# Recurrence keys turned in 32x32 blocks on VectorE and put in place through DRAM, instead of turned on TensorE

## The chip, the cores and the metric

The kernel runs on one core of a Trainium2 chip. Its time is the device time of one execution in microseconds (us). The time of the kernel before is the median of three runs. The trace and the page of the profile come from one execution of their own, which was timed too.

## The reference, cut to what matters

One encoder block over 1024 tokens of width 1024, all in float32. After a layer norm, one wide projection gives the inputs of a dilated attention and of a gated linear recurrence (HGRN2) with eight heads that runs over the tokens forwards and backwards. Both results are merged and projected, and a gated feed-forward layer follows. The change lies in the recurrence. Of it, this part needs the keys with tokens along the contraction:

```python
cum = jnp.cumsum(logf.reshape(b, h, n, c, kd), axis=3)
q_dec = q * jnp.exp(cum)
k_inv = k * jnp.exp(-cum)
a = jnp.einsum('bhnik,bhnjk->bhnij', q_dec, k_inv)
...
u = jnp.einsum('bhnck,bhncv->bhnkv', k * jnp.exp(cum_last - cum), v)
...
_, s_start = lax.scan(step, init, (jnp.moveaxis(decay, 2, 0), jnp.moveaxis(u, 2, 0)))
```

`u` is summed over the tokens `c` of a chunk. It is what the states are made of.

## The kernel before

**Stages.** The first stage computes the projection (11776 columns) and, beside it, attention and recurrence; later stages compute the merge, the output projection and the feed-forward layer. The first stage lasts from the start to about 1190 us; the recurrence's heads lie between 110 and 930 us of it.

**The stream of products.** `stream` yields 322 products. One product is twelve matmuls of 128x128 by 128x512 (four blocks of the contraction, three parts of a split float32 product: lines 277, 278, 279, called by `mm3`). Each yield of `stream` is one *slot*; slots and products are counted alike here, from 0. After certain products a result leaves PSUM (`leave`, at once by priority) through VectorE or ScalarE into a tile `evh`, and SyncE stores that tile to DRAM (lines 578, 598, 609, 628).

**The side work.** In `phase1` the loop over `stream` moves a second generator, one unit at a time: `hgrn_side` for each of eight heads, and attention. A number that `hgrn_side` yields is the number of slots until it is taken up again. A unit starts when its inputs have been produced. Slots give a priority; the scheduler of the framework then sets a fixed order of instructions for each engine. At run time each engine works through its order and waits where an input isn't there.

**One head.** `hgrn_dir` (two directions, `d` 0 and 1) makes the decayed queries `qd` and keys `ki` in place in tile `t` with ScalarE, VectorE (scans, line 1189; reciprocals, line 1207) and GpSimd (line 1197, and line 1210, which finishes the keys). A tile `t` holds eight chunks of 128 tokens as keys x tokens. `hgrn_keys` turns each half of four chunks with four TensorE transposes (line 1224, moving operand the identity in `tabs_sb`) into one PSUM tile `sd`, and ScalarE copies it to `hkT` (line 1225). `hgrn_states` multiplies the turned keys with the values `hv` (line 1240, four and three chunks a direction; the trace has two records for each of these matmuls), scales them on ScalarE (line 1242) and chains them on VectorE and ScalarE (lines 1248, 1251). `hgrn_scores` and `hgrn_out` follow. In slots from the head's start: the keys of direction 0 are turned in slot 4, its states and the turning of direction 1 stand in slot 7, the states of direction 1 in slot 10, the scores in 13, the outputs in 16.

**Queues.** Nearly all DMAs are issued by SyncE (SP) in order: the weight blocks `wa` (line 256), the stores of `evh`, the read-backs of what was stored. A DMA that waits for its input holds up all that stand behind it in SP's order. The instructions of `hgrn_side` that issue DMAs are the fetch of `hv` at its start and of `hg` (line 816) in slot 9.

Of the kernel before, what the change touches and what calls it, by code (L numbers as in the profile page):

```python
# [10 lines left out]
F32 = mybir.dt.float32  # L11
# [11 lines left out]
HALF = 512  # L23
# [56 lines left out]
class Block:  # L80
    evac_ahead = 1000

    def __init__(self, ctx, tc, x, ln_in_g, ln_in_b, w_in, hgrn_lb, hgrn_norm_g, w_att_up, w_hgrn_up,
                 w_o, ln1_g, ln1_b, w_ffn_in, w_ffn_out, ln2_g, ln2_b, tabs, out, dbg=None):
        self.tc, self.nc, self.ctx = tc, tc.nc, ctx
        self.x = x[0]
        self.ln = {"in": (ln_in_g, ln_in_b), "1": (ln1_g[0], ln1_b[0]), "2": (ln2_g[0], ln2_b[0])}
        self.w_in, self.lbw, self.ng = w_in[0], hgrn_lb, hgrn_norm_g[0]
        self.wa, self.wr, self.wo = w_att_up[0], w_hgrn_up[0], w_o[0]
        self.wfi, self.wfo, self.tabs, self.out = w_ffn_in[0], w_ffn_out[0], tabs, out[0]  # L90
        self.dbg = dbg or {}
        nc = self.nc

        self.npj = 0
        self.issued = {}
        self.psum = ctx.enter_context(tc.tile_pool(name="psum", bufs=1, space=PSUM))
        self.cst = ctx.enter_context(tc.tile_pool(name="cst", bufs=1))
        self.tiny = ctx.enter_context(tc.tile_pool(name="tiny", bufs=1))
        self.spare = self.pad(self.cst, CST_PAD)
        self.wpool = self.pool("wp", "right")  # L100
        self.wp = self.wpool.__enter__()
        dram = ctx.enter_context(tc.tile_pool(name="dram", bufs=1, space=DRAM))

        def scratch(name, n):
            if name in self.dbg:
                return [self.dbg[name][i] for i in range(n)]
            return [dram.tile([128, 1024], F32, name=f"{name}{i}") for i in range(n)]

        self.att_d = scratch("att", 4)
        self.rec_d = scratch("rec", 8)  # L110
        self.tg_d = scratch("tg", 16)
        self.n1_d = scratch("n1", 8)
        self.ahs_d = scratch("ahs", 8)
        self.hg_d = [{n: dram.tile([128, T], F32, name=f"hg{h}{n}") for n in ("t0", "t1", "q")}
                     for h in range(8)]
        self.at_d = [{(k, g): dram.tile([128, T], F32, name=f"at{j}{k}{g}") for k in "qk" for g in range(3)}
                     for j in range(4)]
        for h in range(8):
            self.hg_d[h].update({n: dram.tile([T, 128], F32, name=f"hg{h}{n}") for n in "vg"})
        for j in range(4):  # L120
            self.at_d[j].update({("v", g): dram.tile([T, 128], F32, name=f"at{j}v{g}") for g in range(3)})
        self.w_d = [dram.tile([32, 128], F32, name=f"wd{j}") for j in range(4)]
        self.td = [dram.tile([128, 4, HALF], F32, name=f"td{i}") for i in range(3)]
        self.gd = {p: dram.tile([128, NF // 2, HALF], F32, name=f"gd{p}") for p in range(1, 8)}
        self.consts()
# [686 lines left out]
    def fetch_rows(self, n, name, src, g=0):  # L812
# [14 lines left out]
                        self.nc.sync.dma_start(t.rearrange("p (r e) d -> p r e d", e=2)[p:p + 32, :, e], z[i, h, e])  # L827
        return t

    def att_small(self, n, w=8):  # L830
        return self.smt.tile([128, 2, w], F32, name=n, tag=n, bufs=1)

# [382 lines left out]
        nc.vector.scalar_tensor_tensor(qd[:, :, near], q3[:, :, near], CQ, qd[:, :, near], op0=OP.mult, op1=OP.mult)  # L1215
        yield

    def hgrn_keys(self, st, d):

        nc, out = self.nc, []  # L1220
        for b in (0, 1) if d == 0 else (1, 0):
            pt, kT = self.ps_sd(), self.half3("hkT")
            for k in range(4):
                nc.tensor.transpose(pt[:, 128 * k:128 * (k + 1)], st["ki", d][:, 4 * b + k, :], self.ident)
            nc.scalar.copy(kT, pt.rearrange("p (k c) -> p k c", k=4))
            out.append(kT)
        return out

    def hgrn_states(self, st, d, kT, vT):


        nc, dec = self.nc, st["dec", d]
        S = self.slot(6 + d, "hS", (8, 128))
        cs = list(range(8)) if d == 0 else list(range(7, -1, -1))
        E = None
        for b in range(2):
# [4 lines left out]
            for jj, c, after in part:  # L1241
                nc.scalar.activation(S[:, after, :], ps[:, jj, :], AF.Copy, scale=dec[:, 0, c:c + 1])
            for jj, c, after in part:
                if E is None:
                    E = S[:, after, :]
                else:
                    En = self.sm.tile([128, 128], F32, name="hR", tag="hR", bufs=3)
                    nc.vector.scalar_tensor_tensor(En, E, dec[:, 2, c:c + 1], S[:, after, :], op0=OP.mult, op1=OP.add)
                    E = En
                if after != cs[1]:  # L1250
                    nc.scalar.activation(S[:, after, :], E, AF.Copy, scale=dec[:, 1, after:after + 1])
                    if after == cs[2]:
                        nc.scalar.activation(S[:, cs[1], :], S[:, cs[1], :], AF.Copy, scale=dec[:, 1, cs[1]:cs[1] + 1])
        return S
# [55 lines left out]
    def hgrn_side(self, h, st):  # L1310
        nc = self.nc
        vT = self.fetch_rows(5, "hv", self.hg_d[h]["v"])
        st["fa"] = self.slot(6, "fa")
        steps = [self.hgrn_dir(h, d, st) for d in range(2)]
        for _ in range(2):
            for z in steps:
                next(z)
                yield 1
        k0 = self.hgrn_keys(st, 0)
        for z in steps:  # L1320
            next(z)
        yield 2
        next(steps[0])
        yield 1
        S = {0: self.hgrn_states(st, 0, k0, vT)}
        k1 = self.hgrn_keys(st, 1)
        yield 2
        next(steps[1])
        sg = self.fetch_rows(8, "hg", self.hg_d[h]["g"])
        yield 1  # L1330
        S[1] = self.hgrn_states(st, 1, k1, vT)
        yield 3
        am = [self.hgrn_scores(st, b) for b in range(2)]
        yield -3
        for b in range(2):
            self.hgrn_out(h, st, b, am[b], vT, S, sg)
# [743 lines left out]
```

## Time and profile before

| | |
|---|---|
| median of 3 runs | 2018.45 us (2018.29 to 2022.23) |
| the profiled execution | 2016.14 us |
| its span, first to last instruction | 2014.3 us |
| ScalarE busy | 932.8 us (46%) |
| GpSimd busy | 990.4 us (49%) |
| DMA packets | 416125, 301.17 MB, of them under 512 B 133153 |

How to read the rows of the profile shown below. PE is TensorE (PEld its weight loads, which overlap it), DVE is VectorE, ACT is ScalarE, POOL is GpSimd, SP is SyncE, and a `q` behind an engine's name means its sequencer, as where it issues a DMA. A row of the timeline gives start and duration in us, engine, source line, operation, output and inputs, and how many like it were merged. Matmuls overlap, so their durations add to more than the time from one start to the next. A row of waits gives who waited for whom, us in total, how often, and the longest. A row of groups gives busy us and mean ns of one, then the idle time of the engine before them. A row of DMA issues gives count, KB each and the median us from issue to landing. A row of windows gives the stretch, then busy us (and instructions) of PE, PEld, DVE, ACT and POOL, the clock granted to TensorE (1.00 is full speed), the busy share of the 16 DMA engines and GB/s.

### The profile page before, as it was taken

How to read it: one execution, taken by the hardware profiler on the slowest of the kernel's cores; microseconds unless marked ns; L12 is line 12 of the kernel's file. 1: busy time of each engine (PE TensorE's matmuls, PEld its weight loads, DVE VectorE, ACT ScalarE, POOL GpSimd, SP SyncE). 2: the span in 40 equal slices, each digit the busy share in tenths (PEclk: the TensorE clock that was granted, in tenths of full speed). 3: DMA queues.
4: the chain of work that ended last, by engine and by line, in shares of the span. 5: the costliest groups of instructions: out<-in, count | busy, mean ns of one | idle time of the engine just before them, and what ended most of it. 6: DMA issues, size and time to landing. Idle time of an engine off the chain costs nothing. (4 is left out here: it accounts for less than half of the span.)

```text
span 2014.3 us, 30896 instructions
## 1 busy us (share of the span) xinstructions
PE 1976.9 (98%) x10718; PEld 1637.0 (81%) x10718; DVE 1360.7 (68%) x2225; ACT 932.8 (46%) x1926; POOL 990.4 (49%) x866
## 2 busy tenths in 40 slices
PE   7999999999999999999999999999999999999998
PEld 5688788888888888888888878887788888888886
DVE  7877646895478855786443256558777776767788
ACT  6654455553645546455554333345333333344541
POOL 6566643665456654566546422244666665620000
PEclk9999999999999999999999999999999999999999
DMA  5545555456455454555546377534434443447533
GB/s 162 141 126 141 155 131 147 134 126 174 114 153 138 133 155 118 151 156 152 141 121 196 117 256 233 158 119 141 142 125 136 147 136 126 146 163 277 167 103 122
DMA packets 416125, 301.17 MB, mean 150 GB/s; under 512 B 133153, under 2 KB 359394, under 8 KB 415970
## 3 DMA queue, kind: packets, MB, share of 16 engines
q1 hardware_dynamic: 410624, 282.14, 47.9%
q10 hardware_dynamic: 5346, 17.08, 2.3%
q8 instruction: 84, 1.38, 0.3%
q14 instruction: 71, 0.58, 0.1%
HBM read 204.96 MB, written 94.18 MB: 149 GB/s over the span
## 5 line engine op out<-in xcount | busy, mean ns | idle before, releaser
L229 POOL TENSOR_TENSOR w_lo<-wa,w_hi 128x512 fp32r<-128x512 f32 x272 | 366.0, 1355 | 247.3 <-ACT w_hi L219 231.2
L219 ACT CAST w_hi<-wa 128x512 fp32r<-128x512 f32 x272 | 168.2, 620 | 232.4 <-PE pj L278 150.5
L229 POOL TENSOR_TENSOR w_lo<-wsum,w_hi 128x512 fp32r<-128x512 f32 x88 | 127.6, 1460 | 111.2 <-PE sd L279 60.7
L229 POOL TENSOR_TENSOR w_lo<-f_raw,w_hi 128x512 fp32r<-128x512 f32 x66 | 101.1, 1540 | 51.8 <-ACT w_hi L219 50.7
L215 POOL TENSOR_TENSOR mv<-mv,mhalf 128x1 f32<-128x1 f32 x16 | 12.6, 790 | 221.7 <-DVE mv L214 218.7
L219 ACT CAST w_hi<-wsum 128x512 fp32r<-128x512 f32 x88 | 54.5, 621 | 116.5 <-PE sd L278 106.7
L219 ACT CAST gwsum<-a_raw 128x512 fp32r<-128x512 f32 (+1 forms) x78 | 48.2, 618 | 112.2 <-PE pj L278 55.5
L277 PE MATMUL pj<-xt1hi,w_hi 128*128 128x512 f32 x252 | 99.3, 394 | 0.7 <-DVE evh L589 0.7
L607 DVE TENSOR_TENSOR evh<-wkeep,pj 128x512 f32<-128x512 f32 x45 | 30.9, 686 | 99.9 <-PE pj L279 60.1
L278 PE MATMUL pj<-xt1lo,w_hi 128*128 128x512 f32 x252 | 98.3, 390 | 0.0
L279 PE MATMUL pj<-xt1hi,w_lo 128*128 128x512 f32 x252 | 98.1, 390 | 0.0
L727 POOL TENSOR_TENSOR wa<-wa,wa 128x512 f32<-128x512 f32 x46 | 66.8, 1452 | 58.5 <-DVE wa L726 55.2
L229 POOL TENSOR_TENSOR w_lo<-ws,w_hi 128x512 fp32r<-128x512 f32 x46 | 62.1, 1352 | 61.7 <-ACT w_hi L219 57.8
L755 ACT COPY wkeep<-pj 128x512 f32<-128x512 f32 x136 | 79.4, 584 | 0.1
L229 DVE TENSOR_TENSOR gwkeep<-a_raw,gwsum 128x512 fp32r<-128x512 f32 (+1 forms) x78 | 53.0, 680 | 36.5 <-ACT gwsum L219 33.6
L279 PE MATMUL pj<-xt2hi,w_lo 128*128 128x512 f32 x192 | 75.3, 392 | 1.7 <-POOL w_lo L229 1.7
L277 PE MATMUL pj<-xt2hi,w_hi 128*128 128x512 f32 x192 | 75.9, 396 | 0.8 <-ACT w_hi L219 0.8
L278 PE MATMUL pj<-xt2lo,w_hi 128*128 128x512 f32 x192 | 75.5, 393 | 1.2 <-DVE xt2lo L409 1.0
L229 POOL TENSOR_TENSOR w_lo<-w_raw,w_hi 128x512 fp32r<-128x512 f32 x24 | 33.5, 1398 | 87.8 <-ACT w_hi L219 87.8
L277 PE MATMUL pj<-xt4hi,w_hi 128*128 128x512 f32 x192 | 75.9, 395 | 0.0
L278 PE MATMUL pj<-xt4lo,w_hi 128*128 128x512 f32 x192 | 75.3, 392 | 0.0
L278 PE MATMUL pj<-xb11lo,w_hi 128*128 128x512 f32 x192 | 75.3, 393 | 0.0
(440 smaller groups left out, 6536.2 us busy)
## 6 DMA issues: line engine op xcount, KB each, us to landing
wa<-in_w_in_dram SPq DMA_DIRECT2D x184, 256.0 KB, 3.4
f_raw<-in_w_ffn_in_dram SPq DMA_DIRECT2D x44, 512.0 KB, 4.3
a_raw<-gd SPq DMA_DIRECT2D x30, 512.0 KB, 3.9
gd<-fc SPq DMA_DIRECT2D x44, 256.0 KB, 2.0
gd<-fs SPq DMA_DIRECT2D x33, 256.0 KB, 2.2
tg<-evh SPq DMA_DIRECT2D x32, 256.0 KB, 3.4
tg<-tg SPq DMA_DIRECT2D x16, 512.0 KB, 4.8
y<-ahs SPq DMA_DIRECT2D x16, 512.0 KB, 7.5
```

Source lines behind the costliest of these rows:

```text
L215: nc.gpsimd.tensor_tensor(mv[:, 2:3], mv[:, 2:3], self.mhalf[:, 0:1], OP.pow)
L219: ins = nc.scalar.copy(hi, src) if eng_hi == "act" else nc.vector.tensor_copy(hi, src)
L229: ins = e.tensor_sub(lo, src, hi.bitcast(F32))
L277: nc.tensor.matmul(ps, whi, xhi, start=first, stop=False, **kw)
L278: nc.tensor.matmul(ps, whi, xlo, start=False, stop=False, **kw)
L279: self.product = nc.tensor.matmul(ps, wlo, xhi, start=False, stop=last, **kw).ins.name
L607: self.left(nc.vector.tensor_add(t, add, ps))
L727: nc.gpsimd.tensor_sub(a["a21"], a["a22"], a["a11"])
L755: nc.scalar.copy(t, ps)
```

## The change

`hgrn_keys` no longer uses TensorE, PSUM and ScalarE. VectorE turns each half of `t` in 32x32 blocks (`flipped`, one instruction of 128x512), which turns every block but leaves the blocks where they were. The tile is stored to a DRAM scratch `kd` as it is (`stored`, 256 KB) and read back into itself by four DMAs (`back`, 64 KB each), one for each band of 32 partitions, in runs of 32 numbers (128 B), so that the blocks come to their places. For the 16 directions these are 32 such turns, 32 stores and 128 read-backs.

The slots of a head change with it. The keys are turned in slot 3 (direction 0) and 4 (direction 1), stored in slots 4 and 5, read back in 6 and 7; the states stand in slots 10 and 12, the scores in 15, the outputs in 18.

```diff
+        self.kd = [[dram.tile([128, HALF], F32, name=f"kd{h}{n}") for n in range(4)] for h in range(8)]
...
+    def flipped(self, t, scr, src=None):
+
+        self.nc.vector.transpose(t, t if src is None else src)
+        return t, scr
+
+    def stored(self, flips):
+        for t, scr in flips:
+            self.nc.sync.dma_start(scr, t)
+
+    def back(self, flips):
+        for t, scr in flips:
+            z = scr.rearrange("(a i) (k b j) -> b i k a j", a=4, b=4, j=32)
+            for b in range(4):
+                self.nc.sync.dma_start(t[32 * b:32 * b + 32, :].rearrange("i (k a j) -> i k a j", a=4, j=32), z[b])
...
-    def hgrn_keys(self, st, d):
-
-        nc, out = self.nc, []
-        for b in (0, 1) if d == 0 else (1, 0):
-            pt, kT = self.ps_sd(), self.half3("hkT")
-            for k in range(4):
-                nc.tensor.transpose(pt[:, 128 * k:128 * (k + 1)], st["ki", d][:, 4 * b + k, :], self.ident)
-            nc.scalar.copy(kT, pt.rearrange("p (k c) -> p k c", k=4))
-            out.append(kT)
-        return out
+    def hgrn_keys(self, h, st, d):
+        return [self.flipped(self.half("hkT"), self.kd[h][2 * d + b],
+                             st["ki", d][:, 4 * b:4 * b + 4, :].rearrange("p k c -> p (k c)"))
+                for b in ((0, 1) if d == 0 else (1, 0))]
...
-        for _ in range(2):
-            for z in steps:
-                next(z)
-                yield 1
-        k0 = self.hgrn_keys(st, 0)
+        next(steps[0])
+        yield 1
+        next(steps[1])
+        yield 1
+        next(steps[0])
+        yield 1
+        k0 = self.hgrn_keys(h, st, 0)
+        next(steps[1])
+        yield 1
+        self.stored(k0)
+        k1 = self.hgrn_keys(h, st, 1)
         for z in steps:
             next(z)
-        yield 2
+        yield 1
+        self.stored(k1)
+        yield 1
+        self.back(k0)
         next(steps[0])
         yield 1
-        S = {0: self.hgrn_states(st, 0, k0, vT)}
-        k1 = self.hgrn_keys(st, 1)
-        yield 2
+        self.back(k1)
         next(steps[1])
         sg = self.fetch_rows(8, "hg", self.hg_d[h]["g"])
-        yield 1
-        S[1] = self.hgrn_states(st, 1, k1, vT)
+        yield 3
+
+        def turned(keys):
+            return [t.rearrange("p (k c) -> p k c", k=4) for t, _ in keys]
+
+        S = {0: self.hgrn_states(st, 0, turned(k0), vT)}
+        yield 2
+        S[1] = self.hgrn_states(st, 1, turned(k1), vT)
         yield 3
```

The new lines move the numbers of the lines behind them: 256, 277 to 279 and 598 become 257, 278 to 280 and 599, and 1240 becomes 1250.

TensorE's order at the first head, before, at the first keys (in product 32), at the first states and the second keys (both between products 34 and 35):

```order
L277 MATMUL pj<-xt2hi,w_hi 128x512
L1224 MATMUL sd<-tabs_sb,t_1224 128x128 x8
L278 MATMUL pj<-xt2lo,w_hi 128x512
...
L279 MATMUL pj<-xt1hi,w_lo 128x512
L1240 MATMUL sd<-hv,hkT 128x128 x7
L1224 MATMUL sd<-tabs_sb,t_1228 128x128 x8
```

And now, where the second direction's states stand (four inside product 41, three behind the first matmul of product 43, with the first scores, line 1275, right behind them):

```order
L1250 MATMUL sd<-hv,hkT 128x128 x4
...
L278 MATMUL pj<-xb11hi,w_hi 128x512
L1250 MATMUL sd<-hv,hkT 128x128 x3
L1275 MATMUL sd<-qd,t_1256 64x128
L1276 MATMUL sd<-qd,t_1256 64x64
```

The transposes are gone; the seven matmuls of a direction stand in two groups, each behind its own read-backs. That is so in 14 of the 16 directions.

SP's order at the same head, before; `wa` are weight blocks, `hg1g`, `hg1v`, `at0q`, `at0k` stores of the stream's results:

```order
L598 DMA hg1v<-evh 32x16x32 x4
L578 DMA at0q_140<-evh 128x512
L256 DMA wa_1312<-in_w_in_dram 128x4x128
L256 DMA wa_1336<-in_w_in_dram 128x4x128
L256 DMA wa_1420<-in_w_in_dram 128x4x128
L256 DMA wa_1444<-in_w_in_dram 128x4x128
L256 DMA wa_1514<-in_w_in_dram 128x4x128
...
L598 DMA hg1g<-evh 32x16x32 x4
L578 DMA at0k_143<-evh 128x512
```

And now:

```order
L844 DMA hkT<-kd_179 32x16x32 x3
L838 DMA kd_182<-hkT 128x512
L844 DMA hkT<-kd_179 32x16x32
L838 DMA kd_181<-hkT 128x512
L844 DMA hkT<-kd_180 32x16x32 x4
L257 DMA wa_1482<-in_w_in_dram 128x4x128
L599 DMA hg1g<-evh 32x16x32 x4
L579 DMA at0k_143<-evh 128x512
L844 DMA hkT<-kd_182 32x16x32 x4
L599 DMA hg1v<-evh 32x16x32 x4
L844 DMA hkT<-kd_181 32x16x32
L579 DMA at0q_140<-evh 128x512
```

Three more read-backs of `kd_181` follow the last row; with them the last three states above have their keys. The read-backs stand among stores of the stream's results and weight loads, and the stores of direction 1 (`kd_182`, `kd_181`), which wait for its turned keys, stand between read-backs of direction 0.

## The prediction

> **What bounds the kernel now.** I read the page first, then the waits of TensorE, then its timeline at one set of keys, then the queues.
>
> ```profile
> span 2014.3 us, 30896 instructions
> PE 1976.9 (98%) x10718; PEld 1637.0 (81%) x10718; DVE 1360.7 (68%) x2225; ACT 932.8 (46%) x1926; POOL 990.4 (49%) x866
> ```
>
> TensorE is busy in 1976.9 of 2014.3 us. Whatever takes time out of its order shortens the kernel, and whatever makes it wait lengthens it by as much. Nothing else bounds the whole. But the other engines are close in places:
>
> ```profile
> 100.00:1100.00 1000.00, 991.19 (x6344) 828.25 (x6343) 659.12 (x1243) 519.38 (x1227) 569.16 (x526) 1.00 0.53 142
> 650.00:700.00 50.00, 47.85 (x298) 39.96 (x297) 43.85 (x49) 26.47 (x61) 34.69 (x32) 1.00 0.45 127
> ```
>
> Over the stretch with the heads TensorE loses only 8.8 of 1000 us, at full clock, and VectorE is busy two thirds of the time. While a head is under way (second row) VectorE stands at 43.85 of 50. What TensorE waits for there:
>
> ```profile
> PE sd L1240 <- ACT hkT L1225: 3.5, 3, 1.7
> PE sd L1265 <- ACT hS L1242: 2.6, 1, 2.6
> PE sd L1224 <- POOL t L1210: 0.4, 1, 0.4
> ```
>
> The states wait 3.5 us for ScalarE's copies of the turned keys, the transposes 0.4 us for the keys.
>
> **What goes.** One set of eight transposes in TensorE's timeline (two halves of one direction; 16 such sets):
>
> ```profile
> 657.49 0.39 PE L277 MATMUL pj<-xb22hi,w_hi 128*128 128x512 f32 x1
> ...
> 659.99 0.39 PE L279 MATMUL pj<-xb22hi,w_lo 128*128 128x512 f32 x1
> 660.21 0.39 PE L277 MATMUL pj<-xt4hi,w_hi 128*128 128x512 f32 x1
> 660.44 1.03 PE L1224 MATMUL sd<-tabs_sb,t 128*128 128x128 f32 x8
> 661.23 0.47 PE L278 MATMUL pj<-xt4lo,w_hi 128*128 128x512 f32 x1
> 661.54 0.39 PE L279 MATMUL pj<-xt4hi,w_lo 128*128 128x512 f32 x1
> ...
> 666.58 1.72 PE L1240 MATMUL sd<-hv,hkT 128*128 128x128 f32 x14
> 668.05 0.48 PE L277 MATMUL pj<-xb11hi,w_hi 128*128 128x512 f32 x1
> ```
>
> Starts, not durations, count here. A product's twelve matmuls take 660.21 - 657.49 = 2.72 us, 0.227 each. From the first L277 to L279 two steps would take 0.45; they take 661.54 - 660.21 = 1.33. So eight transposes cost 0.87 us of TensorE's order, and 16 sets **13.9 us**. This is sure, since the instructions are gone and TensorE was full. With them go the waits for the keys and for ScalarE's copies, 3.5 + 0.4 = **3.9 us**. Together 17.8 us.
>
> ScalarE also loses 32 copies:
>
> ```profile
> L1225 ACT COPY hkT<-sd x32: 562/593/665, 126.8 to 917.7; 128x512 f32<-128x512 f32 x32
> ```
>
> 32 by 0.593 is 19 us. ScalarE is at 46%, so I cost that at nothing; it may make the copies of the states' results a little earlier.
>
> **What comes.** On VectorE 32 turns of 128x512. The stream's own turns have that shape:
>
> ```profile
> L589 DVE STREAM_TRANSPOSE evh<-evh 128x512 f32<-128x512 f32 x30 | 20.8, 693 | 0.4
> ```
>
> 0.693 us each, 22.2 us in all, 2.8 us a head. They are hidden by VectorE's idle time except inside a head. There a result of the stream that leaves late can hold TensorE: a PSUM bank is written again three products (8.2 us) after the result in it is complete. So VectorE may slip a few us before that costs anything. Without this cover it would cost 22 us.
>
> On SP 32 stores and 128 read-backs. Rows of the same sizes:
>
> ```profile
> hg0t<-evh SPq DMA_DIRECT2D x4, 256.0 KB, 2.2
> hg1g<-evh SPq DMA_DIRECT2D x8, 64.0 KB, 3.3
> at0v<-evh SPq DMA_DIRECT2D x24, 64.0 KB, 2.0
> ...
> 127.56 1.95 SPq L598 DMA_DIRECT2D hg1v<-evh  x4
> ```
>
> A 64 KB piece in runs of 128 B costs SP 1.95/4 = 0.49 us and lands after 2.0 to 3.3 us. These are stores; no read-back in 128 B runs is in the trace. I take 2.3 (the 24 pieces are the larger group) and keep 4.0, a little over the slower row, as the other end. What the engines move then:
>
> ```profile
> 128.50:130.00 1.50, 1.50 (x8) 1.21 (x7) 1.50 (x2) 0.35 (x1) 1.50 (x1) 1.00 0.83 124
> 133.00:135.00 2.00, 2.00 (x20) 2.00 (x19) 2.00 (x2) 1.07 (x2) 1.26 (x1) 1.00 1.07 297
> ```
>
> The first stretch holds four such pieces: 124 GB/s at a DMA share of 0.83. The second holds weight loads: 297. The short runs thus fill the engines, but a half's four read-backs only for some 2 us. All 128 take 128 x 0.5 = 64 us of the engines, spread over eight heads, and enter the sum only through their landing. The Trainium skill (DMA: Bandwidth & Descriptors, Specifications) asks for 512 B or more for line rate; by that rule the landings would be at the 4.0 end, and the new waits below nearer to 28 than to 10. The trace agrees in rate (124 against 297 GB/s), but not in landing: 2.0 us for 24 pieces of 128 B runs.
>
> **The new path.** From finished keys to states there were eight transposes and a copy. Now: two turns 1.39, two stores issued and landed about 0.8 + 2.2, eight read-backs 8 x 0.49 = 3.9, the last landing 2.3: **10.6 us**, and more if VectorE or SP is taken. Six slots are given for it (turn in slot 3, states in 10, where before it was 4 and 7). In the seventh head, direction 0, the keys are late already:
>
> ```profile
> 842.90 1.29 POOL L1210 TENSOR_TENSOR t<-t,qd 128x512 f32<-128x512 f32 x1
> ...
> 844.24 1.09 PE L1224 MATMUL sd<-tabs_sb,t 128*128 128x128 f32 x8
> ```
>
> Keys are finished at 842.90 + 1.29 = 844.19, TensorE takes them at 844.24: no room. This was in product 231. In the new order the head's scores stand at product 244 where they stood at 238; two of these six products are the head's own longer schedule, so the same point comes at product 235, and the states stand at 239. Four products are 10.9 us: 10.6 against 10.9, before any queueing. A reciprocal on VectorE ahead of the turn makes it late.
>
> The other limit is SP's order. At the first head the last three read-backs stand behind the store of product 39 (`at0q`), and the last three states behind three further products, one matmul and four states: 3 x 2.72 + 0.23 + 4 x 0.21 (by 668.05 - 666.58 = 1.47 for seven in the row above) = 9.2 us after product 39. The same kind of store in the trace of before:
>
> ```profile
> 123.64 0.39 PE L279 MATMUL pj<-xb21hi,w_lo 128*128 128x512 f32 x1
> 150.42 0.39 PE L279 MATMUL pj<-xb22hi,w_lo 128*128 128x512 f32 x1
> ...
> 129.61 0.45 SPq L578 DMA_DIRECT2D at0q<-evh  x1
> 153.78 0.74 SPq L578 DMA_DIRECT2D at0q<-evh  x1
> ```
>
> They were issued 3.0 us (150.81 to 153.78) and 5.6 us (124.03 to 129.61) after their products' ends. Behind that come 0.7 for the store, two more issues 1.0 and the landing 2.3: 7.0 or 9.6 us, against 9.2. With a landing of 4.0 it is 8.7 or 11.3.
>
> So the read-backs come about when they are needed, some 2 us early to 2 us late. I counted the 32 groups so: in about 12 the last read-back is late by up to 1.4 us, and the worst of each head adds to 6 us. Delays scatter and only late ones count: 3 us more. TensorE's row is also broken once more in 14 directions, at 0.08 us (661.23 to 661.54 is 0.31 where 0.23 is normal): 1 us. New waits: **10 us**, an estimate; its ends are 0 (all early) and 28 (3.5 us a head, both directions late by nearly 2).
>
> **Sum** against the profiled execution: -13.9 - 3.9 + 10 = -7.8, from 2016.14 to 2008.3 (span 2006.5). The median shown is 2.3 above that execution, so 2018.45 - 7.8 = **2010.6 us**.
>
> **Rivals.**
>
> *All read-backs early*: 2018.45 - 17.8 = 2000.6. For it: ScalarE is freed, and TensorE waited for unfinished keys in one place only (the row of line 1224 above), so most keys are finished with time to spare. Against it: the two counts above leave no room.
>
> *Given back wholly*: VectorE slips. Its 2.8 us a head fall where it is busy 88%; results leave later, so stores on SP too, and the read-backs behind them. If each head loses 1 us more than forecast, waits are 18 and the time is 2018.6. For it speaks that SP already hangs on such results:
>
> ```profile
> SPq L598 <- DVE evh L589: 77.8, 25, 12.3
> SPq L256 <- POOL w_lo L229: 154.2, 77, 7.7
> ```
>
> Up to 12.3 us at once. Against it: TensorE hardly noticed.
>
> *Slower: the round trip lies open.* Place: the states, with everything of the stream behind them on TensorE. It decides from 17.8/8 = 2.2 us a head. At 28 us the time is 2018.45 + 10.2 = 2028.6. It needs read-backs landing at 4 us or more or SP held once more a head, for instance by the store of `kd_182`, which waits for turned keys in front of a read-back and weight blocks. The Trainium skill (VectorE: DVE Perf Modes, Rules for kernel authors) says to turn 128x128 on TensorE where PSUM will do as the target; by that rule this change would lose and the time would be this rival's, and by the rows above the forecast's. The trace agrees with the rule only so far as TensorE's turn is cheap (0.87 us for eight).
>
> That the change does not do what it says, turning without TensorE, can be left out: the new order has no transposes there.
>
> **Chances.** Forecast 0.42, all early 0.15, given back 0.24, slower 0.19. A measurement can tell about 0.2% (4 us) from no change. Faster by more: 0.42 + 0.15 = 0.57; within: 0.24; slower: 0.19. The range goes from 1999, a little below the all-early time, to 2027, short of the open round trip's 28 us; it leaves out about 0.05 below and 0.13 above.
>
> **What would show it.** Right: no line 1224 on TensorE, its busy time down by about 14 us, the turns at about 0.69 us, waits of the states for DMAs (`hkT<-kd`) of some 10 us, spread in pieces of 1 to 2 us over the heads. Wrong: pieces of 4 us and more there; waits for weights (w_hi, w_lo) between 110 and 930 us, which would say that SP's order has pushed the weight blocks back; results that leave so late that a product waits for its bank; read-backs landing far from 2.3 us. A forecast that misses low would have its error in the 10 us; the 13.9 can't miss by more than 1.

## The result and the profile after

| | before | after |
|---|---|---|
| median (runs taken together) | 2019.99 us (2018.29 to 2022.23) | 2038.24 us (2036.06 to 2040.75) |
| the profiled execution, its span | 2016.14, 2014.3 us | 2040.75, 2038.9 us |

The ratio is 1.0097, 95% interval 1.0075 to 1.0119: slower by 15 to 24 us, where 2010.6 us was forecast and the range ended at 2027.

The head of the page after:

```profile
span 2038.9 us, 30944 instructions
PE 1976.5 (97%) x10590; PEld 1630.0 (80%) x10590; DVE 1379.6 (68%) x2257; ACT 919.4 (45%) x1894; POOL 990.9 (49%) x866
```

128 matmuls are gone (10718 to 10590), but TensorE's busy time has hardly moved (1976.9 to 1976.5), and the span is 24.6 us longer. So idle time has come, and something has also lengthened the work that is left. The same stretch of windows as before shows how much idle time lies among the heads (columns as in the prediction):

```profile
100.00:1100.00 1000.00, 966.08 (x6112) 800.36 (x6111) 671.03 (x1271) 496.02 (x1180) 556.09 (x518) 0.99 0.59 154
```

Idle is 1000 - 966.08 = 33.9 us, where it was 8.8: 25.1 more. The granted clock is 0.99 where it was 1.00. TensorE's waits after:

```profile
PE sd L1250 <- DMA hkT<-kd: 17.9, 15, 4.0
...
PE sd L1278 <- ACT hS L1252: 3.8, 2, 2.7
PE pj L280 <- POOL w_lo L230: 3.6, 4, 1.8
PE pj L278 <- DVE evh L590: 3.1, 2, 2.4
PE pj L278 <- DVE evh L624: 2.9, 3, 1.4
...
PE pj L278 <- DVE evh L608: 1.9, 1, 1.9
PE pj L278 <- DVE evh L578: 1.7, 1, 1.7
```

These rows are of the whole span. The waits for ScalarE's copies and for unfinished keys (3.9 us) are gone. In their place the states wait 17.9 us for read-backs, in 15 pieces of up to 4.0. And products wait for PSUM banks whose results VectorE took out late: the rows with `evh`, with one of 0.5 not shown, add to 10.1 us, where they were 1.2; all 8.9 that came lie inside the window. There the waits for `hS` went from 3.2 (two rows, 2.6 and 0.6) to 3.8, those for `w_lo` from 1.2 to 2.5. The sum, -3.9 + 17.9 + 8.9 + 0.6 + 1.3 = 24.8, is nearly all of the 25.1 us of idle time that came.

**The longest wait** shows how the round trip stretches. TensorE's and SP's timelines at the second direction of the sixth head, and the two turns in VectorE's (start, duration, engine, line; idle time before it and its cause in brackets):

```profile
705.00 1.29 DVE L833 STREAM_TRANSPOSE hkT<-t 128x512 f32<-128x512 f32 x2
...
705.72 0.34 SPq L838 DMA_DIRECT2D kd<-hkT  x1
706.16 1.21 SPq L257 DMA_DIRECT2D wa<-in_w_in_dram  x1
707.46 0.47 SPq L838 DMA_DIRECT2D kd<-hkT  x1
708.02 0.38 SPq L807 DMA_DIRECT2D q<-at2q  x1
708.50 0.62 SPq L257 DMA_DIRECT2D wa<-in_w_in_dram  x1
709.18 0.60 SPq L807 DMA_DIRECT2D q<-at2q  x1
710.63 1.28 SPq L844 DMA_DIRECT2D hkT<-kd  x2
711.96 3.18 SPq L599 DMA_DIRECT2D at2v<-evh  x4
715.18 1.92 SPq L844 DMA_DIRECT2D hkT<-kd  x3
```

```profile
713.91 0.39 PE L279 MATMUL pj<-xt4lo,w_hi 128*128 128x512 f32 x1
718.31 2.05 PE L1250 MATMUL sd<-hv,hkT 128*128 128x128 f32 x8 [4.02 <-DMA hkT<-kd]
720.01 0.77 PE L280 MATMUL pj<-xt4hi,w_lo 128*128 128x512 f32 x1
720.58 0.63 PE L278 MATMUL pj<-xt4hi,w_hi 128*128 128x512 f32 x1
```

The two turns took 0.65 us each. The first half's store was issued at once, at 705.72, and it landed after 4.9 us, with five other DMAs issued meanwhile. Two of the half's read-backs went out at 710.63; then four stores of the stream's results took SP 3.18 us; the other two went out from 715.18, and TensorE got its keys at 718.31, 13 us after the turn began.

**The clock.** The windows of four stretches after that:

```profile
716.50:723.30 6.80, 4.47 (x17) 3.81 (x18) 0.69 (x1) 1.14 (x4) 0.00 (x0) 0.50 0.73 171
624.40:627.80 3.40, 3.40 (x10) 2.66 (x9) 3.40 (x6) 1.06 (x2) 3.33 (x3) 0.50 0.45 113
972.50:979.30 6.80, 6.22 (x61) 5.30 (x61) 1.97 (x5) 3.48 (x12) 0.00 (x0) 0.50 0.88 189
167.00:170.40 3.40, 3.40 (x19) 2.79 (x15) 2.92 (x6) 1.72 (x4) 1.28 (x1) 0.50 1.01 351
```

The column behind POOL's is the granted clock: 0.50. Each stretch follows a long wait: the 4.0 us above, 1.9 for an `evh`, 2.3 for read-backs, 2.7 for an `hS`. They are all there are between 100 and 1200 us, 20.5 us together; before the change there was one of 3.4 us, behind the 2.6 us wait for `hS`. In these stretches a product's matmuls start 0.43 us apart (at 624.80, 625.23, 625.66), where 0.23 is usual, so work takes about twice as long. TensorE was busy for 17.5 of the 20.5 us (3.2 of the 3.4 before), so (17.5 - 3.2) / 2 = some 7 us are lost to the clock. This is a good part of what filled the busy time up again.

**The account**, trace against trace: over the whole span TensorE was idle for 62.4 us, where it was 37.4. -13.9 for the transposes, +25.0 idle and some +7 for the clock are +18 of the 24.6. Ahead of 100 us, where no head has begun, the profiled execution after has 3.4 us more at half clock, some 1.7 us that belong to no part of the change. TensorE's broken rows (1.1 us by the prediction's price) and some 4 us not placed are the rest.

### The profile page after: what moved, and what is told of

Its sections match the earlier page's. It is cut to its first block, busy times and chain, and to the rows that moved or that the text cites. A ratio compares the mean times of both kernels' runs of the same rounds, so it can differ in the third digit from the quotient of the medians.

```text
span 2038.9 us, 30944 instructions
## 1 busy us (share of the span) xinstructions
PE 1976.5 (97%) x10590; PEld 1630.0 (80%) x10590; DVE 1379.6 (68%) x2257; ACT 919.4 (45%) x1894; POOL 990.9 (49%) x866
## 5 line engine op out<-in xcount | busy, mean ns | idle before, releaser
L278 PE MATMUL pj<-xb11hi,w_hi 128*128 128x512 f32 x192 | 76.9, 403 | 4.4 <-DVE evh L624 2.6
L280 PE MATMUL pj<-xb11hi,w_lo 128*128 128x512 f32 x192 | 76.5, 399 | 0.0
```

What stands on the lines that cost most here:

```text
L278: nc.tensor.matmul(ps, whi, xhi, start=first, stop=False, **kw)
L280: self.product = nc.tensor.matmul(ps, wlo, xhi, start=False, stop=last, **kw).ins.name
```

## The experiments

All ratios are to runs of the kernel before beside them on the same chip. "Idle" is 1000 us less TensorE's busy time in the window 100 to 1100; "half" is the time at clock 0.50 between 100 and 1200 us. Both, and the waits, are from the one profiled execution of each kernel; the waits are added over its whole span.

| kernel | median us | ratio (95%) | idle | read-back waits | `evh` waits | half |
|---|---|---|---|---|---|---|
| before | | 1 | 8.8 | | 1.2 | 3.4 |
| after | 2038.2 | 1.0097 (1.0075 to 1.0119) | 33.9 | 17.9 | 10.1 | 20.5 |
| e1 no round trip | 2004.0 | 0.9926 (0.9909 to 0.9943) | 10.7 | | 6.9 | 0 |
| e2 ScalarE instead | 2027.0 | 1.0045 (1.0029 to 1.0061) | 27.3 | 17.5 | 6.6 | 13.7 |
| e3 slots alone | 2017.1 | 0.9994 (0.9985 to 1.0003) | 8.8 | | 3.0 | 6.8 |
| e5b states later | 2042.2 | 1.0121 (1.0106 to 1.0136) | 35.3 | 18.3 | 9.4 | 30.7 |
| e6 DMAs first | 2051.7 | 1.0165 (1.0138 to 1.0193) | 41.9 | 9.1 | 9.6 | 20.5 |
| e7 half of it | 2018.5 | 0.9997 (0.9982 to 1.0012) | 16.4 | 6.7 | 6.9 | 10.2 |
| e8 DMAs alone | 2025.3 | 1.0044 (1.0032 to 1.0057) | 9.4 | | 3.4 | 3.4 |
| e9 scores first | 2036.9 | 1.0103 (1.0088 to 1.0118) | 29.4 | 0 | 13.9 | 13.7 |
| e11 its control | 2034.3 | 1.0085 (1.0069 to 1.0102) | 19.9 | | 3.4 | 10.2 |
| e13 buffers alone | 2017.5 | 0.9999 (0.9990 to 1.0009) | 9.9 | | 3.9 | 0 |
| e14 all on ScalarE's queue | 2029.0 | 1.0061 (1.0045 to 1.0078) | 25.6 | 9.0 | 10.2 | 10.2 |
| e15 stores on ScalarE's queue | 2033.3 | 1.0092 (1.0067 to 1.0117) | 29.1 | 16.8 | 7.0 | 37.5 |
| e16 into a spare tile | 2017.5 | 0.9995 (0.9984 to 1.0005) | 9.1 | | 3.4 | 3.4 |
| e17 stores alone | 2014.6 | 0.9978 (0.9967 to 0.9988) | 9.5 | | 4.9 | 0 |
| e18 half, on ScalarE's queue | 2013.8 | 0.9977 (0.9966 to 0.9988) | 11.1 | 1.0 | 6.6 | 3.4 |

Diffs are against the changed kernel where nothing else is said.

### Is the gain real, and which part gives it back? (e1, e2, e3)

```diff
# e1
-        for t, scr in flips:
-            self.nc.sync.dma_start(scr, t)
...
-        S = {0: self.hgrn_states(st, 0, turned(k0), vT)}
+        S = {0: self.hgrn_states(st, 0, [vT[:, 0:4], vT[:, 4:8]], vT)}
```

> The changed kernel without its stores and read-backs: VectorE still turns the keys, and the states take the values in place of the keys (so the states are not the reference's, and they wait for no key). Theory A (the round trip through DRAM lies open: TensorE waits 17.9 us for read-backs, and the slower clock behind the longest waits adds some 8 us): those waits are gone, the time falls from 2038 to about 2012, below the kernel before by about 8 us. Theory B (VectorE slips: its turns make results of the stream leave late, 9.6 us of waits for evh): these waits stay at 7 us or more. Theory C (SP's order with the added DMAs pushes weight loads back): the wait for w_lo (2.5 us after 100 us) goes to below 1 us.

The VectorE turns stay, the DMAs are gone, and nothing waits for them: the states take the values in place of the keys, so they are not the reference's. 2003.95 us, 8 less than Theory A had named. TensorE's window and its waits:

```profile
100.00:1100.00 1000.00, 989.31 (x6267) 823.84 (x6267) 679.90 (x1281) 513.02 (x1209) 583.17 (x538) 1.00 0.53 145
```

```profile
PE pj L280 <- POOL w_lo L230: 4.0, 6, 1.1
PE pj L278 <- ACT w_hi L220: 3.6, 3, 2.0
PE pj L278 <- DVE evh L590: 2.2, 2, 1.5
PE pj L278 <- DVE evh L624: 2.0, 2, 1.0
```

The gain is there: 11.5 to 18.4 us by the interval (13.4 by the medians), and idle is 10.7. After 100 us no wait is over 1.5 us, and among the heads the clock is full. The DMAs and what waits for them thus cost 34 us from here to the kernel after.

```diff
# e2
-        self.nc.vector.transpose(t, t if src is None else src)
+        self.nc.scalar.activation(t, t if src is None else src, AF.Copy, scale=0.0)
```

> The changed kernel with ScalarE writing zeros into the key tile (from the same source, after the same wait) where VectorE turned it; stores, read-backs and slots stay, the keys of the states are zero. VectorE is relieved of 22 us, ScalarE has its former load. Theory A: the waits of the states for read-backs stay at 10 us or more and the time between 2024 and 2036. Theory B: the waits for evh between 360 and 900 us go from 9.6 us to under 3 us, and if that is the main cause the time is below 2020.

Here ScalarE writes zeros into the tiles and VectorE is spared; the DMAs stay. The read-back waits stay too:

```profile
PE sd L1250 <- DMA hkT<-kd: 17.5, 12, 3.8
```

The waits for `evh` fall from 10.1 to 6.6 us, idle by 6.6, half clock by 6.8 (3.4 us of time): 10 us, and the medians differ by 11.3. So some 11 of the 34 us need VectorE's turns as well as the DMAs; the DMAs without the turns still make the gain a loss. Of the `evh` waits neither is the whole cause: 6.9 us stand with the turns alone (e1), 6.6 with the DMAs alone (e2), 10.1 with both.

```diff
# e3
+                nc.tensor.transpose(pt[:, 128 * k:128 * (k + 1)], st["ki", d][:, 4 * b + k, :], self.ident)
+            nc.scalar.copy(kT, pt.rearrange("p (k c) -> p k c", k=4))
...
-        self.stored(k0)
...
-        self.back(k0)
```

> The kernel before with only the new slots of a head (keys turned on TensorE in slots 3 and 4, states in 10 and 12, scores 15). Theories A, B and C: no DMA and no VectorE work is added, so the time is that of before within 4 us (2016 to 2024), rather lower since the copies of the keys come long before the states. Rival D (the new order of the side work itself costs): 2028 or more.

TensorE's keys in the new slots: no difference from before. The longer head costs nothing by itself.

### Can another place in the order hide the round trip? (e5b, e6, e9, e11, e13)

```diff
# e5b: both directions' states in slot 13
-        yield 3
+        yield 6
...
+        S[1] = self.hgrn_states(st, 1, turned(k1), vT)
         yield 2
-        S[1] = self.hgrn_states(st, 1, turned(k1), vT)
-        yield 3
```

> The changed kernel with the states of both directions in slot 13 (they were in 10 and 12), scores and outputs as they are in the changed kernel, so the length of a head stays. Theory A: the waits for read-backs fall from 17.9 us to 8 us or less, and the time to between 2016 and 2028. Theory B: the waits for evh stay and the time stays above 2030. A cost of its own: scores and outputs stand closer behind the states, so waits for hS may grow by some 4 us.

A miss: 18.3 us of waits, now in 10 pieces of up to 5.7, and 30.7 us at half clock. Direction 1 had moved only by one slot, direction 0 by three. Why the waits did not shrink is not shown; one reading is that the scheduler again put the states where it reckoned the read-backs to come, with nothing to spare.

```diff
# e6
+            with self.tc.high_priority(offset=self.evac_ahead):
+                self.nc.sync.dma_start(scr, t)
```

> The changed kernel with stores and read-backs of the keys raised in priority, so that SP's order has them ahead of stores of the stream's results and weight loads that it had behind. If most of the lateness is SP's order, the waits for read-backs fall from 17.9 us to under 9 us and the time to 2022 to 2030. If it is the length of the hops themselves (store to landing 2 to 6 us, then eight issues and a landing), the waits stay at 13 us or more and the time above 2032.

The same was done for the read-backs. Their waits halve to 9.1 us, but TensorE now waits 9.0 us for `w_hi` (2.0 in the kernel after), 6.4 for `w_lo` (3.6) and 5.5 for `hS` (3.8), idle is 41.9, and the time rises to 2051.7 us, where 2022 to 2030 was expected with waits that short. SP's order is a budget: what goes ahead takes from the weight blocks behind it.

```diff
# e9 (SMT_PAD 0, six half buffers, two hR)
+        am = [self.hgrn_scores(st, b) for b in range(2)]
+        yield 3
         S = {0: self.hgrn_states(st, 0, turned(k0), vT)}
...
-        yield 3
-        am = [self.hgrn_scores(st, b) for b in range(2)]
```

> The changed kernel with scores ahead of the states (slot 10 instead of 15; they need no turned keys), states of direction 0 in slot 13 and of direction 1 in slot 15 (they were in 10 and 12), outputs in 18 as they are. One more buffer for halves, one less for the chain of states, and a pad left out to make room. In the order the states then stand in their slots, none pushed back behind its read-backs and none in two groups. Theory A (the states' place in the order is too near behind the read-backs, and the slow clock follows the waits): waits for read-backs under 4 us, no slow clock between 100 and 1200 us, time 2006 to 2014. Theory C (the added DMAs cost some 8 us by themselves): waits gone, but 2014 to 2021. If later states only move the waits, as in the run with the states 3 slots later: 2030 or more. Outputs may wait for hS by up to 5 us.

With the scores ahead the states stand in slots 13 and 15, and every read-back is early. The time is still 2036.9 us:

```profile
PE sd L1302 <- ACT hS L1261: 9.3, 4, 3.8
...
PE pj L278 <- DVE evh L624: 4.0, 3, 1.9
PE pj L280 <- POOL w_lo L230: 3.6, 5, 1.5
PE pj L278 <- DVE evh L590: 3.1, 2, 2.4
```

The slack was taken from the chain of states, whose end `hS` the outputs now wait for (9.3 us).

> The control to it: the same slots and buffers with the keys turned on TensorE, no DMA and no VectorE turns added. All theories: 2013 to 2022, as the kernel before. If the order with scores first is faster by itself, this shows it.

The control, e9's order and buffers with TensorE's keys as in e3, has no round trip and still stands at 2034.3 us, where 2013 to 2022 was expected by all theories. Its largest wait among the heads is not for `hS`:

```profile
PE sd L1285 <- DVE qd L1231: 5.8, 5, 2.7
```

With two smaller rows the scores wait 10.0 us for the decayed queries `qd`: they now come before VectorE has finished these. So with the scores first the change costs 2.5 us by the medians (the intervals overlap), and the order 17.9.

> The keys by TensorE in the slots of the changed kernel, the states ahead of the scores as there, but six half buffers instead of five, two hR buffers instead of three and no padding. It splits the 18 us that the scores-first order with TensorE keys cost. Theory A (that cost comes from the order: scores in slot 10, states in 13 and 15): this kernel stands like the slots alone, 2015 to 2020 us, waits of TensorE for qd near nothing. Theory B (it comes from the buffers, two hR above all): 2028 us or more, with the waits for qd or for outputs' tiles still there.

e11's buffers with e3's order: 0.9999. The cost lies in the order, not in the buffers by themselves.

### Is it the DMAs' traffic? (e8, e16, e17)

```diff
# e8, against e3
+        f0 = [(t.rearrange("p k c -> p (k c)"), self.kd[h][n]) for n, t in enumerate(k0)]
+        self.stored(f0)
...
+        self.back([(self.ke[h][n], scr) for n, (_, scr) in enumerate(f0)])
```

> Keys turned on TensorE in the new slots (the kernel that ran at 2017.1), with the changed kernel's 32 stores and 128 read-backs added in the changed kernel's slots, the read-backs going to a second DRAM scratch that nobody reads. So SP issues the same DMAs, the engines move the same runs of 128 B, and nothing waits for them. Theory A (the cost is the wait of the states for the round trip): the time stays within 4 us of 2017. Theory C (the added DMAs in SP's order, or their traffic, hold up weight loads and results): 2023 or more, with waits for w_lo, w_hi or evh over 8 us after 100 us.

All 160 DMAs run; nobody waits for the read-backs, which end in a second DRAM scratch. 1.0044, 7.3 us by the medians, but the profiled execution was the fastest of nine (2016.8 us, the others from 2023.6) and shows no new wait, so neither theory fits: the time is Theory C's, without its waits. Two further kernels took it apart.

```diff
# e16, against e8
-        self.back([(self.ke[h][n], scr) for n, (_, scr) in enumerate(f0)])
+        self.back([(self.sink(), scr) for _, scr in f0])
```

To make room for the tile, padding in memory (SMT_PAD) and one of the three `hR` buffers are left out, as in e13.

> TensorE's keys in the changed slots; the 32 stores and 128 read-backs run beside them, the read-backs into a spare tile that nobody reads (in place of the third hR buffer and the padding). With read-backs into a second DRAM scratch the same traffic cost some 7 us that the profiled execution did not show. Theory A (those 7 us belong to reads that end in DRAM, twice the DRAM traffic): this kernel stands at 2015 to 2020 us, and the changed kernel's loss is all waits and half clock. Theory B (the traffic and its issue on SP cost that much by themselves): 2022 us or more, and 7 us of the changed kernel's loss would be there without any wait for a key.

> TensorE's keys in the changed slots and the 32 stores of 256 KB, no read-back at all. Theory A (the small runs of the read-backs are what costs in the traffic-only kernel): 2015 to 2019 us. Theory B (the stores, 8 MB more written to DRAM, cost): 2021 us or more.

Into a tile, as in the changed kernel, the traffic costs nothing (0.9995). The loss of e8 went with the reads that end in DRAM; why they cost was not seen in a trace. So the changed kernel's loss isn't its bytes, nor the time SP takes to issue them, by themselves; it needs what waits for them. The stores alone stand 0.2% below before, although they only add work: so much a new order of the same work seems to bring by itself, which is to be kept in mind for e18.

### Is it the queue? (e7, e14, e15, e18)

```diff
# e14; in e15 the first pair alone
-            self.nc.sync.dma_start(scr, t)
+            self.nc.scalar.dma_start(scr, t)
...
-                self.nc.sync.dma_start(t[32 * b:32 * b + 32, :].rearrange("i (k a j) -> i k a j", a=4, j=32), z[b])
+                self.nc.scalar.dma_start(t[32 * b:32 * b + 32, :].rearrange("i (k a j) -> i k a j", a=4, j=32), z[b])
```

> The changed kernel with the 32 stores and 128 read-backs issued by ScalarE's queue instead of SP's. Theory A (the read-backs came late because SP issues everything in one order, the store behind loads that wait and the sixteen read-backs 0.65 us apart): the waits for read-backs fall from 17.9 us to under 8, and the time comes below 2035. Theory B (the two hops are long by themselves, store landing 2 to 5 us and read-back landing 2 to 4): the waits stay above 12. ScalarE then waits for the store's landing ahead of each half's read-backs, so that its copies come late: waits for hS and for ScalarE's evh over 8 us, and 2035 to 2050.

```profile
PE sd L1250 <- DMA hkT<-kd: 9.0, 8, 2.5
...
PE pj L278 <- DVE evh L624: 3.8, 3, 1.9
PE pj L278 <- DVE evh L590: 3.1, 2, 2.4
PE sd L1278 <- ACT hS L1252: 3.0, 3, 2.1
```

The time falls below 2035, as Theory A said; the waits fall by half, not quite to its 8. The issue rows of the kernel after (first two) and of e14 say that the landings are not the reason:

```profile
kd<-hkT SPq DMA_DIRECT2D x32, 256.0 KB, 2.6
hkT<-kd SPq DMA_DIRECT2D x128, 64.0 KB, 2.7
```

```profile
kd<-hkT ACTq DMA_DIRECT2D x32, 256.0 KB, 3.4
hkT<-kd ACTq DMA_DIRECT2D x128, 64.0 KB, 3.4
```

On ScalarE's queue both landings are longer (median 3.4 us against 2.6 and 2.7), and yet TensorE waits less for the keys. So what stretched the round trip was to a good part the place in SP's order.

> The changed kernel with the 32 stores alone on ScalarE's queue; the read-backs stay on SP. Theory A (the store held on SP makes the round trip late): read-back waits from 17.9 us to 8 to 12, time 2025 to 2034. Theory B (the read-backs' issue and landing and the order that puts the states right behind them set the wait): read-back waits 14 to 20 and 2034 to 2042.

With the stores alone moved, 16.8 us of read-back waits stay, as Theory B said, and the ratio is that of the changed kernel within its interval. (The median, 2033.3 us, lies just inside the time that Theory A gave.) In the kernel after, the stores do hold SP up, since they wait for the turned keys:

```profile
SPq L838 <- DVE hkT L833: 26.2, 12, 12.3
```

With the stores off SP this hold is gone, and the waits stay. So it is the read-backs' place on SP that counts; no run moved them alone. The profiled execution was 10 us longer than the three others (2032.9 to 2033.6) and has 37.5 us at half clock, so its row of the table is no typical one.

```diff
# e7; e18 is e7 with e14's queues
-        k1 = self.hgrn_keys(h, st, 1)
...
-        self.stored(k1)
...
-        self.back(k1)
...
+        k1 = self.hgrn_keys_pe(st, 1)
+        yield 2
```

> Only direction 0 goes through VectorE and DRAM, with its states in slot 12; direction 1, whose keys are finished last, is turned on TensorE in slot 10. Theory A: 7 us of transposes go (half of 13.9), the waits for read-backs, which lie mostly in direction 1 (13 of 18 us) and for direction 0 get two slots more, fall under 3 us: 2009 to 2016, the first to beat the kernel before while it computes the reference. If direction 0 waits as much as before (5 us) and VectorE's slip stays: 2017 to 2022.

Direction 0 goes through DRAM and has its states two slots later, direction 1 is turned by TensorE (in slot 10). Level with before; 6.7 us of read-back waits in three pieces stand against the half gain of 7.0.

> Direction 0 by VectorE and DRAM with the states in slot 12, direction 1 by TensorE in slot 10, and the stores and read-backs on ScalarE's queue. With them on SP this stood level with the kernel before (ratio 0.9997) and had 6.7 us of read-back waits in 3 pieces. Theory A (SP's order makes them late): read-back waits under 3 us, 2009 to 2015 us, ratio 0.996 to 0.998, which would be faster than both kernels. Theory B (half of the change has as much VectorE slip and lateness as it gains): 2016 to 2021, ratio 0.999 to 1.002.

With the queue changed to ScalarE's, all three numbers came as Theory A had them: read-back waits 1.0 us, 2013.8 us, ratio 0.9977.

```profile
PE sd L1261 <- DMA hkT<-kd: 1.0, 1, 1.0
```

```profile
100.00:1100.00 1000.00, 988.90 (x6302) 825.09 (x6301) 669.13 (x1262) 519.14 (x1220) 574.44 (x534) 1.00 0.57 152
```

This is a version that beats both kernels: half the transposes are 8 x 0.87 = 7.0 us, and 4.6 us arrive (2.4 to 6.9 by the interval). But the stores-alone kernel beside it shows that 0.2% may come from the order alone, so how much of it is the transposes' isn't settled.

## Why the prediction was wrong, by its own steps

- **"-13.9" and "-3.9": right.** No transposes and no waits for keys' copies are left, and e1, where the saving stands alone, is 13.4 us faster. It still has 6.9 us of `evh` waits.
- **"The turns" at 0.693 us: right in duration, wrong in price.** They took 0.669 us on average. They were costed at nothing, under cover of idle time and of 8.2 us of tolerance in the PSUM banks. The cover did not hold: results left late and TensorE waited for its banks (10.1 us against 1.2). e2, without the turns, is 11 us faster than the kernel after; the turns without the DMAs (e1) have 6.9 us of these waits. This is the rival "given back wholly", with its mechanism (VectorE slips inside the heads).
- **"New waits: 10 us": the step that failed.** It was 17.9. The hops came near the median rows it was built on (stores 2.6 against 2.2, read-backs 2.7 against 2.3), but it added medians where the end is set by the slowest: a store that landed after 4.9, four other stores of 3.18 us between a half's read-backs. A read-back also took SP 0.63 us to issue (median), not 0.49, so eight take 5.1 us, not 3.9. The count "some 2 us early to 2 us late" allowed for 1.4 us of lateness, the trace has 4.0. The list of signs named "pieces of 4 us and more" as what would show it wrong. e14 shows that the place in SP's order made about half of it (9.0 left), though landings there are longer.
- **The clock: not in the sum at all.** A wait was priced at its own length. Four of the waits were followed by 3.4 or 6.8 us at half clock, some 7 us more.
- **The rival "round trip lies open"** had the right sign and place, and a price of 28 us of new waits. Its conditions were not met as it named them: the read-backs landed in 2.7 us, not 4, and with the stores that hold SP moved away (e15) the waits stayed. All new waits together came to about its price (17.9 + 8.9 + 0.6 + 1.3 = 28.7), but only 17.9 were its own, so that this fits is luck. The clock came on top. Its time, 10.2 us over before, fell short by 8: the medians are 18.3 apart.
- **"The new slots" cost nothing: right** (e3), as was that the extra traffic costs nothing but its landing (e16). By the rule of 512 B (the Trainium skill, DMA: Bandwidth & Descriptors, Specifications) the landings were to be at the 4.0 end; the median was 2.7.

The rule quoted from the Trainium skill (VectorE: DVE Perf Modes, Rules for kernel authors), to turn 128x128 on TensorE, gave the sign here. By the runs its reason here is the path back to place, not the turn: the turn alone (e1) was the faster one.

## What to carry to other kernels

On a full engine a cheap instruction is worth its time, and an asynchronous replacement is worth it only if its *latest* arrival is early: price a round trip through DRAM by the slowest landing and by everything that stands between its DMAs on their queue, not by medians. Price a wait of TensorE with the clock behind it. A queue that is full of other work makes DMAs late that are fast by themselves; try another engine's queue before another slot, since a later slot takes its slack from the chain behind it (e9), and what moves ahead for it from the chain in front (e11).

## What the runs showed of the hardware

Two of TensorE's rows after, each behind a wait (in brackets):

```profile
379.36 0.50 PE L278 MATMUL pj<-xb21hi,w_hi 128*128 128x512 f32 x1 [2.40 <-DVE evh L590]
...
623.84 0.47 PE L278 MATMUL pj<-xb11hi,w_hi 128*128 128x512 f32 x1 [1.86 <-DVE evh L608]
```

The stretches at half clock begin on a grid of 3.41 us: from 167.0 to 624.4 are 134 such steps, from there to 716.5 are 27, to 972.5 another 75. What decides whether one begins is the idle time inside one step of the grid. The wait of 1.86 us before 623.84 lay in one step and was followed by half clock; the longer one of 2.40 us before 379.36 was divided by the grid (at 378.6) into some 1.6 and 0.8 and was not. In the 17 traces together, between 100 and 1200 us, every step at full clock with 2 us or more of idle time was followed by half clock, and none with 1.7 us or less was; in between both occur. This does not say how long a stretch lasts: the one from 972.5 went on for a second step, though in its first TensorE was idle for only 0.58 us. The Trainium skill (TensorE: Matmul & The Clock Gate, Why this matters for your kernels) warns of gaps over about 3 us. The trace agrees in the half clock behind a gap, but gaps from 1.9 us on already cost it here.
